# Expert slots in blocks of 32: seven groups of 128 in place of eight pairs and a part of 64

## The chip, the core and the metric

One NeuronCore of a Trainium2 chip runs the whole program in one launch. The metric is device time in microseconds of one execution. TensorE (PE, with its weight loads as PEld), VectorE (DVE), ScalarE (ACT), GpSimd (POOL) and SyncE (SP) each work through their own queue in order; 16 DMA engines move data between HBM and SBUF. Most loads are issued from SyncE's queue, a few from GpSimd's and ScalarE's.

## What is computed

Two residual layers over 256 tokens of width 1024 and a final RMSNorm. Each layer has a mixer (attention) and a mixture of 16 experts of hidden width 512, of which every token takes two. All is float32. The part that the change touches, from the reference:

```
aff = sigmoid(xf @ router_w)                       # 256 x 16
# per token: the best of 4 groups of 4 experts, in it the best 2 experts, weights w normed to 1
...
hid = silu(xb @ w_gate[e]) * (xb @ w_up[e])        # 1024 -> 512, for the tokens xb of expert e
ys  = hid @ w_down[e]                              # 512 -> 1024
out = out.at[tok].add(ys * w)                      # then x = x + gate_f * out
```

An expert has three matrices of 2 MB; all 16 are read in both layers, 100.7 MB a layer. How many tokens an expert gets depends on the data.

## The kernel before

`moe` (L957) runs once a layer, as the second half. It makes the router's values on DVE, and for each token and expert a position among the expert's tokens (`pos`) and a weight (`Wt`), both in `route` (L1030).

**Slots.** Every expert gets CAP = 64 slots. `pick` (L1042) compares `pos` with 0 to 63 and so makes a 0/1 matrix tokens x slots. `gather` (L1050) multiplies it with the tokens (8 chunks of 128 features, four matmuls each) and writes the gathered, scaled tokens to `XG`; it works for four experts (a quad, 256 columns) at a time. One expert of the first twelve, that with most tokens, is exchanged by `places` (L1348) for expert 4 (BIG) and gets 64 slots more, as a part of its own: `XG_x`, `x_hidden` (L1300), `x_slots`, `x_transposed`, `x_down` (L1328), worked in pair 4 (`self.more`, L1202). `rounds` (L1382) works out which tokens are still over, and `rest` (L1441) holds a conditional on their number: each round would load one expert's weights again for 64 tokens. `rest` reserves six ring tiles for that (L1442) and branches on PE, ACT, DVE and SP.

**Pairs.** Experts are worked in eight pairs (L1193), 64 slots of one on PSUM partitions 0 to 63, of the other on 64 to 127, so that a matmul has 64 columns of weights (the gathered tokens) and streams 512 columns of an expert's matrix. A pair does `hidden` (gate, then up, `gate_up` L1084: 8 chunks x 2 sides x 2 matrices), `slots` (`by_slot` L1111: transposes the 0/1 matrix to `OT` and brings the token weights to the slots), `turn` (`transposed` L1102), and, after the `hidden` of the next pair, `rows` (`down` L1135, then the weighting `rows_of` L1140); `combine` (L1128) adds the result to X. Each float32 matmul stands in the trace as two records. The very last pair ends with `finish` (L1272) in three pieces of columns, with the final norm behind them.

**Order and loads.** The loop at L1460 goes over the pairs; quads are gathered while pairs before them are worked. The conditional stands ahead of pair 4. Weights come in tiles of 1 MB into a ring of 15 slots (RING + EXTRA, L28): a pair has four tiles for gate, four for up and four for down. The program's order of loads is gate and up of a pair, then down of the pair before. Pairs 0 and 1 are always experts 12 to 15, so that their loads are issued without knowing the routing; the experts of later pairs are read from `ex_p` (L1346) into a register of SyncE (pair 4: of GpSimd, L1205), behind which SyncE's later loads stand. A scheduler orders each engine's instructions when the program is built; nothing passes the conditional.

**The shape with 32 columns** is in the program already: `ada_chunk` (L312) multiplies with weights of 32 columns, on the four quarters of a bank in turn (L322).

Of the kernel before, what the change touches and what calls it, by code (L numbers as in the profile page):

```python
# [29 lines left out]
QUADS = 3, 2, 1, 0  # L30
BIG = 4 * QUADS[2]


def shape_constants():
# [40 lines left out]
    iota = np.tile(1000 + np.arange(64, dtype=f)[None], (P, 1))  # L75
# [4 lines left out]
    sets = [[("ident", ident), ("iota", iota), ("rank", rank), ("sel", sel)],  # L80
# [17 lines left out]
def trunk(ctx, tc, ins, out):  # L98
# [858 lines left out]
    def moe(cp, wk, layer, norm, end):  # L957
# [73 lines left out]
        pos, Wt, cnt, ids = route[:, 0:2], route[:, 2:4], route[:, 4], route[:, 5]  # L1031
# [10 lines left out]
        def pick(o, at):  # L1042

            n = at.shape[2]
            iota = const("iota")[:, 0:CAP].unsqueeze(1).to_broadcast([P, n, CAP])
            for t in range(2):
                vec.tensor_tensor(o[:, t].rearrange("p (e s) -> p e s", e=n), iota,
                                  at[:, t].unsqueeze(2).to_broadcast([P, n, CAP]), ALU.is_equal)

        def gather(parts, o):  # L1050

            n = sum(m for _, m in parts)
            for k in range(8):
# [4 lines left out]
                at = 0  # L1058
                for XG, m in parts:
                    if (k + at // 256) % 2:  # L1060
                        act.activation(XG[:, k, :], b[:, at:at + m], AF.Identity, bias=sh[:, k:k + 1], scale=fa[:, k:k + 1])  # L1061
                    else:
                        vec.tensor_scalar(XG[:, k, :], b[:, at:at + m], fa[:, k:k + 1], sh[:, k:k + 1], ALU.mult, ALU.add)
                    at += m
# [15 lines left out]


        sides_ = (1, 0)

        def gate_up(XG, c0, Wg, Wu):  # L1084
# [93 lines left out]
        def pick_tile():  # L1178
            return wk.tile([P, 2, 6 * CAP], F32R, tag="pick", name="pick")

        def picked(q):
            o = pick_tile()
            pick(o[:, :, 0:4 * CAP], pos[:, :, 4 * q:4 * q + 4])
            if q == BIG // 4:
                pick(o[:, :, 4 * CAP:6 * CAP], at_b.unsqueeze(2).to_broadcast([P, 2, 2]))
            return o, q == BIG // 4

        def gathered(o, big_):
            XG = hp.tile([P, 8, 4 * CAP], F32, tag="HT", name="XG")
            gather([(XG, 4 * CAP)] + [(XG_x, CAP)] * big_, o)  # L1190
            return o, XG

        class Pair:  # L1193


            def __init__(self, i, o, XG):
                q, pp = QUADS[i // 2], i % 2
                self.first, self.last = i == 0, (layer, i) == (1, 7)
                self.after = i == 4
                self.o, self.XG, self.pp = o, XG, pp  # L1200
                self.e0 = 4 * q + 2 * pp
# [7 lines left out]
            def hidden(self):  # L1209
                names = ("moe_w_gate", "moe_w_up")  # L1210
                if self.first:
                    W = [load_both(nm, self.e0) for nm in names]
# [559 lines left out]
```

## Time and profile before

| | us |
|---|---|
| runs shown (3): lowest, median, highest | 897.03, 897.13, 898.13 |
| the profiled execution | 896.29 |
| its span, first to last instruction | 894.6 |
| busy: PE, PEld | 809.9, 417.0 |
| busy: DVE, ACT, POOL | 402.7, 250.2, 114.2 |
| moved by DMA | 291.09 MB, mean 325 GB/s |

All times in the text are microseconds from the start of the span of this one execution. A busy engine works on an instruction; matmuls overlap, and the end of each is modelled. Layer 0's experts run from about 227 to 490, layer 1's from about 632 to the end.

### The profile page before, as it was taken

Reading aid. Unit: us, or ns where it says so; the run is one execution under the profiler, and the core shown is the slowest. Engines: PE = TensorE matmul, PEld = TensorE weight load, DVE = VectorE, ACT = ScalarE, POOL = GpSimd, SP = SyncE. Lnnn points to the kernel's source line nnn. Section 1 sums busy time; section 2 is a strip of 40 time slices with the busy share of each in tenths; the row PEclk is TensorE's granted clock in tenths of the full one; section 3 lists DMA queues with packets and bytes.
Section 4 is the critical chain, followed back from the end, with each engine's and each line's share of the span. In section 5 each row is a group of like instructions: output and inputs, shape, how many; then the busy total and the mean of one; then the engine's idle time right before and its main releaser. Section 6 shows DMA issues by size and latency. Waiting matters only on the chain. (4 is left out here: it accounts for less than half of the span.)

```text
span 894.6 us, 12020 instructions
## 1 busy us (share of the span) xinstructions
PE 809.9 (91%) x4371; PEld 417.0 (47%) x4371; DVE 402.7 (45%) x1119; ACT 250.2 (28%) x595; POOL 114.2 (13%) x118
## 2 busy tenths in 40 slices
PE   4699999998999887999998799887999987999996
PEld 1298666555434333434332568555434333434333
DVE  2385777777623213124225754876613314115214
ACT  1264555545102001102012354546102112002113
POOL 1020211233000001000001223444000001000001
PEclk9799999998999998999999999989899999999998
DMA  9999869789899956999997977729699977999951
GB/s 326 343 342 386 301 233 272 282 310 368 314 421 400 406 205 253 419 419 420 397 406 257 337 267 204 297 104 362 226 421 421 419 282 280 419 418 419 415 197 47
DMA packets 84840, 291.09 MB, mean 325 GB/s; under 512 B 9174, under 2 KB 23202, under 8 KB 63010
## 3 DMA queue, kind: packets, MB, share of 16 engines
q1 hardware_dynamic: 76976, 258.36, 76.1%
q0 software_dynamic: 4608, 29.37, 8.5%
q10 hardware_dynamic: 3186, 2.47, 0.9%
q8 instruction: 38, 0.62, 0.3%
q14 instruction: 32, 0.26, 0.1%
HBM read 289.12 MB, written 1.06 MB: 324 GB/s over the span
## 5 line engine op out<-in xcount | busy, mean ns | idle before, releaser
L1078 PE MATMUL o<-slot,hT 128*64 128x512 f32 (+1 forms) x368 | 103.2, 611 | 7.7 <-PEq L1449 7.7
L1078 PE MATMUL mm<-slot,XG 128*64 128x512 f32 x328 | 94.2, 606 | 0.0
L1078 PE MATMUL sc<-slot,XG 128*64 128x512 f32 x352 | 90.4, 593 | 0.0
L1099 DVE TENSOR_TENSOR hq<-sc,hid 128x512 f32<-128x512 f32 x16 | 16.9, 1054 | 157.8 <-PE sc L1078 157.8
L497 ACT CAST hl<-slot 128x512 fp32r<-128x512 f32 (+2 forms) x112 | 60.7, 557 | 72.2 <-PE mm L514 45.3
L454 POOL TENSOR_TENSOR hl<-slot,hl 128x512 fp32r<-128x512 f32 x40 | 52.9, 1325 | 162.3 <-ACT hl L497 134.5
L1125 ACT CAST yg<-adac 128x512 fp32r<-128x512 f32 (+1 forms) x34 | 20.9, 613 | 148.3 <-DVE adac L1144 116.9
L1078 PE MATMUL mm<-room,XG 128*64 128x512 f32 x184 | 60.2, 606 | 0.0
L1144 DVE SCALAR_TENSOR_TENSOR adac<-o,w,GATE 128x512 f32<-128x512 f32 (+1 forms) x33 | 24.2, 735 | 77.8 <-PE o L1078 76.0
L1133 DVE TENSOR_TENSOR X<-X,tp 128x512 f32<-128x512 f32 (+1 forms) x72 | 46.2, 677 | 27.5 <-PE tp L1132 27.5
L1078 PEld LDWEIGHTS o<-slot,hT 128*64 128x64 f32 x368 | 31.8, 143 | 55.5 <-issue 51.5
L512 PE MATMUL mm<-HH,hl 128*128 128x256 f32 x176 | 54.5, 311 | 2.3 <-ACT HH L486 2.3
L322 PE MATMUL tp<-slot,csil 128*32 128x512 f32 x344 | 49.7, 655 | 3.7 <-DMA slot<-in_ada_w_dram 3.4
L1078 PEld LDWEIGHTS sc<-slot,XG 128*64 128x64 f32 x352 | 28.7, 137 | 51.3 <-issue 49.8
L1078 PE MATMUL o<-room,hT 128*64 128x512 f32 (+1 forms) x160 | 52.2, 575 | 0.0
L514 PE MATMUL mm<-HH,hl 128*128 128x256 f32 x176 | 50.2, 287 | 0.5 <-DVE hl L454 0.5
L513 PE MATMUL mm<-HH,hl 128*128 128x256 f32 x176 | 50.5, 288 | 0.1
L1132 PE MATMUL tp<-yg,OT 128*128 128x512 f32 (+1 forms) x128 | 42.6, 439 | 8.0 <-ACT yg L1125 4.2
L454 DVE TENSOR_TENSOR hl<-slot,hl 128x512 fp32r<-128x512 f32 (+2 forms) x72 | 42.8, 613 | 15.4 <-ACT hl L497 15.1
L1057 PE MATMUL tp<-pick,XH 128*128 128x256 f32 (+1 forms) x128 | 39.6, 333 | 10.6 <-ACT hT L1108 3.5
L1078 PE MATMUL sc<-room,XG 128*64 128x512 f32 x160 | 46.6, 592 | 0.0
L1057 PEld LDWEIGHTS tp<-pick,XH 128*128 128x128 f32 x128 | 24.5, 192 | 33.7 <-ACT XG L1061 6.7
(410 smaller groups left out, 1377.9 us busy)
## 6 DMA issues: line engine op xcount, KB each, us to landing
slot<-in_ada_w_dram SPq DMA_DIRECT2D x43, 1024.0 KB, 9.5
slot<-in_moe_w_down_dram SPq DMA_DIRECT2D x39, 1024.0 KB, 12.8
slot<-in_moe_w_gate_dram SPq DMA_DIRECT2D x37, 1024.0 KB, 12.7
slot<-in_moe_w_up_dram SPq DMA_DIRECT2D x35, 1024.0 KB, 10.3
room<-in_moe_w_gate_dram SPq DMA_DIRECT2D x19, 1024.0 KB, 9.4
room<-in_moe_w_up_dram SPq DMA_DIRECT2D x19, 1024.0 KB, 11.3
room<-in_moe_w_down_dram SPq DMA_DIRECT2D x13, 1024.0 KB, 10.5
slot<-in_ev_w_in_dram SPq DMA_DIRECT2D x8, 1024.0 KB, 10.2
```

The costliest lines, as they stand in the source:

```text
L322: mm(b[g:g + 32], csil[:, k, 1 - half:33 - half], W[k], start=k < 4, stop=k >= 4)
L454: eng.tensor_tensor(lo, v, hi.bitcast(F32), ALU.subtract)
L497: act.copy(hi, src)
L512: mm(o, a[0], b[0], start=start, stop=False, skip_group_check=True)
L513: mm(o, a[0], b[1], start=False, stop=False, skip_group_check=True)
L514: mm(o, a[1], b[0], start=False, stop=stop, skip_group_check=True)
L1057: mm(b, xk[i][:, t, k, :], o[:, t, 0:n], start=t == i == 0, stop=t == i == 1)
L1078: last[0] = mm(*args, **kw)
L1125: act.copy(yg[:, 0, :], v)
L1132: mm(cb, OT[:, t, :], x, start=i == 0, stop=i == 1)
L1133: vec.tensor_tensor(X[:, t, sl], X[:, t, sl], cb, ALU.add)
L1144: vec.scalar_tensor_tensor(v, y, w, gate[:, sl], ALU.mult, ALU.mult)
```

## The change

CAP stays for the rounds alone. Slots now come in blocks of 32. The first fourteen experts (0 to 13) are sorted on chip by their number of tokens (`places`): for every pair of them a comparison, a sum for the rank, and then six products and sums with a 0/1 matrix, which bring positions, weights, counts and numbers to sorted places (`placed`). The places have fixed sizes: the largest expert gets 96 slots, the next eight 64, the last five 32; experts 14 and 15 are not sorted and have 64. Seven groups of 128 slots take the places of the eight pairs: 14 + 15; 96 + 32; 64 + 32 + 32; 64 + 64; 64 + 32 + 32; 64 + 64; 64 + 64. A group with a 96 or a 32 is worked in four parts of 32 columns, one for each 32 partitions (`blocks`), where an expert of three blocks streams its matrix three times; the other groups are worked in two parts of 64, as before.

The part of 64 for the big expert goes out of the pairs; its functions stay for the rounds. The first gather covers group 0 alone (128 columns) and uses unsorted positions, the later ones two groups each (256 columns). Only group 0's experts are fixed; from group 1 on they are read from `ex_p`. `rounds` stands behind group 0; the conditional stands ahead of group 3 and follows a group of three experts. A load of a group of three experts has six tiles per matrix. The first set of constants has 78 columns more.

The diff, cut to its core:

```
+GROUPS = [[(14, 2), (15, 2)], [(0, 3), (1, 1)], [(2, 2), (3, 1), (4, 1)], [(5, 2), (6, 2)], [(7, 2), (8, 1), (9, 1)],
+          [(10, 2), (11, 2)], [(12, 2), (13, 2)]]
+RANKS = 0, 9, 1, 10, 11, 2, 3, 4, 12, 13, 5, 6, 7, 8
+SORTED = len(RANKS)
+BLOCK = 32
...
+        def blocks(group):
+            ns = [n for _, n in group]
+            if ns == [2, 2]:
+                return [(1, slice(64, 128)), (0, slice(0, 64))]
+            at = [a for a, n in enumerate(ns) for _ in range(n)]
+            return [(at[j], slice(BLOCK * j, BLOCK * j + BLOCK)) for j in reversed(range(4))]
+
+        def gate_up(XG, c0, parts, Wg, Wu):
...
-                    for a in sides_:
-                        put(b[64 * a:64 * a + 64], XG[:, k, c0 + a * CAP:c0 + (a + 1) * CAP], W[a][k], start=k == 0, stop=k == 7)
+                    for a, at in parts:
+                        put(b[at], XG[:, k, c0 + at.start:c0 + at.stop], W[a][k], start=k == 0, stop=k == 7)
...
-        def down(put, y, hT, Wd, k, half):
-            for a in sides_:
-                at = slice(64 * a, 64 * a + 64)
+        def down(put, parts, y, hT, Wd, k, half):
+            for a, at in parts:
...
-                self.more = self.e0 == BIG
-                es = [self.e0, self.e0 + 1]
-                if i > 1:
+                es = list(range(self.p0, self.p0 + self.n))
+                if i:
                     es = [load_value(ex_p[:, e:e + 1], [(ET.SP, ET.Pool)[self.after]], NE - 1) for e in es]
...
-                self.hid = gate_up(self.XG, 2 * CAP * self.pp, *W)
-                if self.more:
-                    self.hx = x_hidden(XG_x, [w[0] for w in W])
+                self.hid = gate_up(self.XG, self.c0, self.parts, *W)
...
-                    vec.tensor_copy(self.w[0:64], wb[0:64, 0:1])
-                    vec.tensor_copy(self.w[64:128], wb[64:128, 1:2])
+                    junk = wk.tile([P, 3], F32, tag="wj", name="wj")[:, 0:self.n]
+                    vec.tensor_tensor_reduce(out=junk, in0=wb, in1=self.owner, scale=1.0, scalar=0.0, op0=ALU.mult,
+                                             op1=ALU.add, accum_out=self.w)
...
-                if self.more:
-                    flush()
-                    late.extend(x_down(self.hTx, self.Wd[0]))
...
+            key = cp.tile([P, n], F32, name="key")
+            vec.scalar_tensor_tensor(key, route[:, 4, 0:n], 16.0, ids[:, 0:n], ALU.mult, ALU.add)
...
+            vec.tensor_tensor(more, key.unsqueeze(1).to_broadcast(wide), key.unsqueeze(2).to_broadcast(wide), ALU.is_gt)
+            rank = cp.tile([P, n], F32, name="rank")
+            vec.tensor_reduce(rank, more, AX.X, ALU.add)
+            vec.tensor_tensor(here, rank.unsqueeze(1).to_broadcast(wide), const("ranks").unsqueeze(2).to_broadcast(wide),
+                              ALU.is_equal)
+            for i in (5, 4, 0, 1, 2, 3):
+                vec.tensor_tensor(more, route[:, i, 0:n].unsqueeze(1).to_broadcast(wide), here, ALU.mult)
+                vec.tensor_reduce(placed[:, i, 0:n], more, AX.X, ALU.add)
+                if i == 5:
+                    vec.tensor_copy(ex_p[:, 0:n], placed[0:1, 5, 0:n])
...
-        now = gathered(*picked(QUADS[0]))
+        o, XG = gathered(*picked([0], route[:, 0:2]))
+        places()
         for h in range(2):
             vec.tensor_scalar(OT_x[:, h], ident.unsqueeze(1).to_broadcast([P, 2, P]), 0.0, None, ALU.mult)
-        at_b = places()
-        rounds()
+        then = picked([1, 2], placed[:, 0:2])
         before = None
-        for i in range(8):
-            p = Pair(i, *now)
-            if i == 4:
+        for i in range(len(GROUPS)):
+            p = Group(i, o, XG, 128 * (i > 0 and i % 2 == 0))
+            if i == 3:
...
-            if i % 2 == 0 and i < 6:
-                o = picked(QUADS[i // 2 + 1])
-            if i % 2 and i < 7:
-                now = gathered(*o)
+            if i % 2 == 0 and i < 5:
+                o, XG = gathered(*then)
+            elif i < 5:
+                then = picked([i + 2, i + 3], placed[:, 0:2])
+            if i == 0:
+                rounds()
```

## Rows read from the trace of the kernel before

**Rows 1.** The page: busy tenths of PE in 40 equal slices of the span (22.4 us each), and what the DMA engines moved in each.

```profile
PE   4699999998999887999998799887999987999996
GB/s 326 343 342 386 301 233 272 282 310 368 314 421 400 406 205 253 419 419 420 397 406 257 337 267 204 297 104 362 226 421 421 419 282 280 419 418 419 415 197 47
```

**Rows 2.** Busy time by stretch: the expert stages up to the branch, from the branch to the landing of the last expert weight, and behind it. Columns: the stretch and its length; busy us (and instructions) of PE, PEld, DVE, ACT, POOL; granted clock of PE; share of the DMA engines; GB/s.

```profile
227.10:351.30 124.20, 109.96 (x512) 45.54 (x513) 39.26 (x105) 17.64 (x34) 2.74 (x5) 0.98 0.84 332
351.30:464.40 113.10, 111.49 (x550) 45.55 (x552) 28.64 (x51) 14.23 (x26) 3.90 (x8) 0.98 1.00 407
464.40:490.00 25.60, 21.92 (x98) 7.64 (x98) 11.62 (x18) 4.00 (x9) 4.95 (x15) 1.00 0.87 301
631.60:749.80 118.20, 107.68 (x515) 45.62 (x514) 39.33 (x105) 17.73 (x34) 2.74 (x5) 0.99 0.84 338
749.80:863.50 113.70, 112.00 (x554) 45.01 (x554) 29.55 (x52) 14.34 (x26) 3.70 (x7) 0.99 1.00 402
863.50:894.60 31.10, 22.34 (x108) 9.46 (x108) 12.75 (x26) 7.75 (x22) 3.88 (x4) 0.91 0.09 35
```

**Rows 3.** SyncE's last issue of an expert load in layer 0 (timeline), its time to landing, and the time to landing of all expert loads of L1160 (minimum, median, maximum).

```profile
454.39 0.33 SPq L1160 DMA_DIRECT2D room<-in_moe_w_down_dram  x1
DMA to landing us min/median/max: 10.0/10.0/10.0
DMA to landing us min/median/max: 5.0/11.5/25.9
```

**Rows 4.** Busy time by stretch (columns as in rows 2) in layer 1, ten us before the branch's end and ten us soon after.

```profile
740.00:750.00 10.00, 5.59 (x22) 3.23 (x24) 4.79 (x11) 1.94 (x4) 0.14 (x1) 0.96 0.47 196
760.00:770.00 10.00, 10.00 (x66) 4.71 (x64) 1.28 (x3) 0.90 (x3) 1.02 (x2) 1.00 1.01 418
```

**Rows 5.** Who waited for whom, PE alone: us in total, times, longest.

```profile
PE o L1078 <- PEq L1449: 7.7, 2, 4.2
PE tp L322 <- DMA slot<-in_ada_w_dram: 3.4, 4, 1.5
```

**Rows 6.** Timeline around layer 0's branch: issues of loads by SyncE (SPq) and GpSimd (POOL). Start, length, what, and for how long and by what the queue stood before it.

```profile
314.92 0.33 SPq L1160 DMA_DIRECT2D slot<-in_moe_w_down_dram  x1
339.35 0.53 POOL L1160 DMA_DIRECT2D slot<-in_moe_w_up_dram  x1
351.40 1.19 POOL L1160 DMA_DIRECT2D slot<-in_moe_w_up_dram  x2 [11.53 <-PEq L1449]
```

**Rows 7.** The chain that ended last, in order of time: one up phase of a pair in layer 1.

```profile
791.53 6.87 PE sc L1078 x32
```

**Rows 8.** Timeline of PE: one `ada_chunk` at the full clock.

```profile
129.74 1.92 PE L322 MATMUL tp<-slot,csil 128*32 128x512 f32 x16
```

**Rows 9.** Busy time in layer 0's stretch up to the branch, of one line's instructions each (PE, then PEld; clock, DMA share, GB/s of the stretch): L1078 (gate, up, down), L1057 (gather), L1132 (combine), L1116 (transposes of slots), L1118 (weights of slots), L1106 (transposes of the hidden values).

```profile
227.10:351.30 124.20, 80.38 (x352) 24.05 (x353) 0.98 0.84 332
227.10:351.30 124.20, 17.87 (x96) 13.17 (x96) 0.98 0.84 332
227.10:351.30 124.20, 8.59 (x24) 3.93 (x24) 0.98 0.84 332
227.10:351.30 124.20, 1.75 (x8) 0.80 (x8) 0.98 0.84 332
227.10:351.30 124.20, 2.02 (x16) 2.10 (x16) 0.98 0.84 332
227.10:351.30 124.20, 2.59 (x16) 1.68 (x16) 0.98 0.84 332
```

**Rows 10.** The branch instructions of the conditional's line on PE's sequencer, two layers: minimum, median and maximum in ns.

```profile
L1449 PEldq COMPARE_BRANCH  x2: 3391/3616/3842, 347.2 to 746.1; - x2
```

**Rows 11.** Layer 0 from the branch to the end of the stage: busy time of L1306 (gate and up of the part of 64) and of L1333 (its down), and the group of its combine (busy us, mean ns of one; idle before).

```profile
351.30:490.00 138.70, 8.45 (x64) 5.14 (x64) 0.98 0.97 387
351.30:490.00 138.70, 5.16 (x16) 1.06 (x16) 0.98 0.97 387
L1132 PE MATMUL tp<-yg,OT_x 128*128 128x512 f32 x8 | 2.4, 420 | 0.0
```

**Rows 12.** Timeline: the last down record of layer 0 on PE and the last two additions to X on DVE; the last piece's matmuls of layer 1.

```profile
484.35 0.59 PE L1078 MATMUL o<-slot,hT 128*64 128x512 f32 x1
488.66 1.29 DVE L1133 TENSOR_TENSOR X<-X,tp 128x512 f32<-128x512 f32 x2 [0.30 <-PE tp L1132]
883.32 1.95 PE L1078 MATMUL o<-room,hT 128*64 128x256 f32 x16
```

**Rows 13.** From layer 0's last expert landing to the first product of layer 1's attention: the stretch (columns as in rows 2), and that product in PE's timeline.

```profile
464.40:501.00 36.60, 29.48 (x143) 10.71 (x140) 21.34 (x39) 8.67 (x19) 6.22 (x16) 1.00 0.86 290
501.02 0.47 PE L512 MATMUL o<-hl,HH 128*128 128x512 f32 x1 [1.58 <-ACT hl L497]
```

**Rows 14.** Timeline of DVE in layer 0: the key, a product on 96 elements, a comparison on 256, and the experts' numbers.

```profile
226.30 0.17 DVE L1357 SCALAR_TENSOR_TENSOR key<-route 128x16 f32<-128x16 f32 x1
228.61 0.26 DVE L1366 TENSOR_TENSOR here<-route,is_max 128x96 f32<-128x96 f32 x1
230.38 0.42 DVE L1047 TENSOR_TENSOR pick<-K,route 128x256 fp32r<-128x256 f32 x1
230.71 0.16 DVE L1372 CAST ex_p<-route 1x16 int32<-1x16 f32 x1
```

**Rows 15.** Busy time by stretch (columns as in rows 2): just behind layer 0's branch.

```profile
351.30:354.00 2.70, 2.69 (x8) 0.94 (x10) 0.60 (x2) 0.00 (x0) 1.59 (x3) 0.50 0.49 109
```

More of the change, by code (lines that the diff above doesn't have):

```diff
@@ L74, in shape_constants @@
     sin = np.tile(np.sin(ang).T, (4, 1)).astype(f)
-    iota = np.tile(1000 + np.arange(64, dtype=f)[None], (P, 1))
+    iota = np.tile(1000 + np.arange(96, dtype=f)[None], (P, 1))
+    ranks = np.tile(np.array(RANKS, f)[None], (P, 1))
+    places = sorted(x for g in GROUPS for x in g)
+    size = np.tile(np.array([BLOCK * n for _, n in places], f)[None], (P, 1))
+    owner = np.concatenate([np.repeat(np.eye(len(g), dtype=f), [BLOCK * n for _, n in g], axis=0) for g in GROUPS], axis=1)
     rank = np.tile((4 - np.arange(4)).astype(f)[None], (P, 1))
@@ L1040, in moe, with pick, gather @@
         gate = GATE[5]
[L1042 removed]
+        def pick(o, at, m):
             n = at.shape[2]
[L1045 removed]
+            iota = const("iota")[:, 0:m].unsqueeze(1).to_broadcast([P, n, m])
             for t in range(2):
                 vec.tensor_tensor(o[:, t].rearrange("p (e s) -> p e s", e=n), iota,
[L1048 to L1052 removed]
+                                  at[:, t].unsqueeze(2).to_broadcast([P, n, m]), ALU.is_equal)
+        def gather(XG, n, o):
             for k in range(8):
@@ L1178, in pick_tile, with picked, gathered, __init__ @@
         def pick_tile():
-            return wk.tile([P, 2, 6 * CAP], F32R, tag="pick", name="pick")
-        def picked(q):
+            return wk.tile([P, 2, 256], F32R, tag="pick", name="pick")
+        def picked(groups, pos):
             o = pick_tile()
[L1183 to L1190, printed above, removed]
-            return o, XG
[L1193 to L1201, printed above, removed]
-                self.more = self.e0 == BIG
-                es = [self.e0, self.e0 + 1]
-                if i > 1:
+            places, at = [x for g in groups for x in GROUPS[g]], 0
+            while places:
+                p0, m = places[0]
+                n = 1
+                while n < len(places) and places[n] == (p0 + n, m):
+                    n += 1
+                pick(o[:, :, at:at + n * m * BLOCK], pos[:, :, p0:p0 + n], m * BLOCK)
+                at += n * m * BLOCK
+                places = places[n:]
+            return o, at
+        def gathered(o, n):
+            XG = hp.tile([P, 8, n], F32, tag="HT", name="XG")
+            gather(XG, n, o)
+            return o, XG
+        class Group:
+            def __init__(self, i, o, XG, c0):
+                self.first, self.last = i == 0, (layer, i) == (1, len(GROUPS) - 1)
+                self.after = i == 3
+                self.o, self.XG, self.c0 = o, XG, c0
+                self.p0, self.n = GROUPS[i][0][0], len(GROUPS[i])
+                self.parts = blocks(GROUPS[i])
+                first = sum(len(g) for g in GROUPS[:i])
+                self.owner = const("owner")[:, first:first + self.n]
+                es = list(range(self.p0, self.p0 + self.n))
+                if i:
                     es = [load_value(ex_p[:, e:e + 1], [(ET.SP, ET.Pool)[self.after]], NE - 1) for e in es]
@@ L1211, in hidden @@
                 if self.first:
-                    W = [load_both(nm, self.e0) for nm in names]
+                    W = [load_both(nm, self.p0) for nm in names]
                 else:
@@ L1294, in moe @@
         NR = 7
-        XG_x = cp.tile([P, 8, CAP], F32, name="XG_x")
         w_x = cp.tile([P, 1], F32, name="w_x")
@@ L1346, in moe @@
         ex_p = cp.tile([1, 16], I32, name="ex_p")
+        placed = cp.tile([P, 6, 16], F32, name="placed")
         def places():
@@ L1358, in places @@
-            vec.memset(is_max, 0.0)
-            free = slice(0, 4 * QUADS[0])
-            vec.tensor_reduce(top_, key[:, free], AX.X, ALU.max)
-            vec.tensor_scalar(is_max[:, free], key[:, free], top_, None, ALU.is_equal)
-            a, b = (cp.tile([P, NR, 16], F32, tag=n, name=n)[:, 0:6] for n in ("here", "here_t"))
-            col = cp.tile([P, 6], F32, name="xcol")
-            wide = is_max.unsqueeze(1).to_broadcast([P, 6, 16])
-            vec.tensor_tensor(a, route, wide, ALU.mult)
@@ L1375, in places @@
-            return at
+            n = SORTED
+            key = cp.tile([P, n], F32, name="key")
+            vec.scalar_tensor_tensor(key, route[:, 4, 0:n], 16.0, ids[:, 0:n], ALU.mult, ALU.add)
+            wide = [P, n, n]
+            more, here = (x[:, 0:n * n].rearrange("p (a b) -> p a b", b=n) for x in (ada_tile(), ada_tile()))
+            vec.tensor_tensor(more, key.unsqueeze(1).to_broadcast(wide), key.unsqueeze(2).to_broadcast(wide), ALU.is_gt)
+            rank = cp.tile([P, n], F32, name="rank")
@@ L1378, in moe @@
+            vec.tensor_copy(placed[:, :, n:16], route[:, :, n:16])
         at_x = cp.tile([P, 2, NR], F32, name="at_x")
@@ L1465, in moe @@
                 rest()
-            if i == 7 and layer:
+            if p.last:
                 end.load()
```

54 lines of the change are left out of this document (16 added, 38 removed).

## The prediction

> **What bounds the kernel now.** I read the slices of the page first [rows 1]: the long stretches where the DMA engines move some 419 GB/s are the two expert stages, and there PE is at nine tenths as well. Busy PE says little, so I cut each stage at its one conditional (`rest`, L1441) and took a table of stretches [rows 2]. The two layers are twins: 124.2 and 118.2 us up to the branch at 332 and 338 GB/s, then 113.1 and 113.7 us to the landing of the last expert weight at 407 and 402 GB/s, then a tail without expert loads of 25.6 us (to the end of the stage in layer 0) and 31.1 us (to the end of the span in layer 1). In layer 0 the landing is 454.4 + 10.0, issue and time to landing of the last load [rows 3]; in layer 1 the stretch behind 863.5 moves 35 GB/s, the 1 MB of the output. In the tens around the branch [rows 4] the loads fall to less than half and return to 418 GB/s for good.
>
> Which of PE and DMA holds each part is read from PE's waits [rows 5]: the list of what PE waited for names loads of `ada_w` (and one constant at the start), never a load of an expert; the expert stage's largest wait is the branch itself. So up to the branch PE is the bound, and the DMA queue waits for PE to free slots. After it the two are matched: DMA is full, and PE has so much queued that it ends 20 us and more after the last landing.
>
> Why DMA sags is seen in the issues [rows 6]: SyncE issues its last load before the branch at 314.92; GpSimd then gets out five tiles, the fifth at 339.35, and the sixth goes at 351.40, released by the branch. The ring has 15 slots, `rest` holds 6 through the branch (L1442) and the previous pair's down weights 4; five are left.
>
> **What the change takes away.** Tokens first, since slots must hold them: the routing of the reference on its inputs gives layer 0 a largest expert of 58 tokens, layer 1 of 71 (expert 0), then 57 (expert 2). Of the fourteen sorted ones ranks 9 to 13 have at most 26 and 20 tokens, experts 14 and 15 at most 30. All fit 96, 64 and 32 slots, so `rest` runs no round, and the trace of before shows none either (no instruction of L1430 to L1439).
>
> One matrix phase (gate, up or down of 128 slots) is 32 matmul records in 6.87 us, two in each 0.43 [rows 7]. Will a group of four 32-slot parts take the same? It has 64 records, in four column groups. The trace has that shape: `ada_chunk` (L322) runs 16 records of 128 rows x 32 columns x 512 in 1.92 us [rows 8]; less the 0.16 us by which a record outlasts its spacing (0.59 [rows 12], against 0.43) that is 0.11 us a record, and 64 make 7.0. I take 6.87; bounds 6.87 and, if only two of the four ran at once, 13.74.
>
> Before the branch: four pairs become three groups, so gate, up and one down go: 3 x 6.87 = 20.6 us. The gathers (L1057, 17.87 us) cover 128 + 256 + 256 in place of 256 + 256 + 320 columns: 17.87 x 192/832 = 4.1. One combine of three: 8.59/3 = 2.9. One of four of the slot transposes, slot weights and hidden transposes: (1.75 + 2.02 + 2.59)/4 = 1.6 [rows 9]. Together 29.2 us a layer. The 14.2 us in which PE was idle there (124.2 - 110.0, [rows 2]) and the 3.4 to 3.8 us of the branch [rows 10] I leave as they are.
>
> After the branch: the overflow part of the big expert goes, 8.45 + 5.16 + 2.4 = 16.0 us [rows 11] and its small transposes. PE's count of pairs stays (four gates, four ups, five downs), so PE needs about 139 - 16 = 123 us there in layer 0.
>
> **What it adds, and what is late next.** A layer has 96 tiles of 1.05 MB. Before, 4 pairs (48 tiles) and GpSimd's five are issued by the branch, and 43 remain: 45.1 MB, and the stretch shows 113.1 x 0.407 = 46.0. After, groups 0 to 2 hold seven experts (42 tiles), and the ring has 15 - 6 - 6 = 3 slots for group 3, so 51 remain: eight more, at 2.50 us each (1.05 MB at 419 GB/s) 20.0 us. From the branch to the last landing thus 133.1 and 133.7 us, more than PE's 123: the second part is held by DMA. Last landing: 29.2 - 20.0 = 9.2 us earlier in each layer.
>
> The tail shrinks, because PE waits for the last tile in place of holding a queue. Layer 0: the last two tiles feed half a down phase (3.43), and from its end (484.94) to the last addition to X (489.95) are 5.0 us [rows 12]: 8.4 for 25.6, that is 17.2 less. Layer 1: half of the last piece (0.97), then from the piece's end (885.27) to the end of the span 9.3: 10.3 for 31.1, 20.8 less. If PE still has a few us queued, that much is lost; bounds 0 and 4 us a layer.
>
> Between the layers a cover goes. The next layer's `ada` and attention weights now land while PE ends layer 0: 36.6 us x 290 GB/s = 10.6 MB from the last expert landing to the first attention product at 501.02 [rows 13]. After, that time is 8.4 + 11.0 = 19.4 us, 8.1 MB at 419; missing are 2.5 MB, 6.0 us. Bounds: 0 (not all of it is wanted by the first product) and 10.0 (all that landed by 490, 7.7 MB, is wanted 8.4 us after the last landing). I take 6.0, since that product is the first to need the new weights.
>
> The sort adds a wait. Before, the eight tiles of pair 0 and seven of pair 1 are loaded ahead of the routing; after, only experts 14 and 15 are fixed, and SyncE's queue stands at group 1's expert numbers, with all later loads behind it. Those come from `ex_p`, which was ready at 230.71 + 0.16, some 4.6 us after its key, after ten small steps among other work [rows 14]. The new chain has compare, sum, equality, product, sum on 196 elements; 96 elements took 0.26 us and 256 took 0.42, so about 0.36 each, 1.8 us together. I keep 231. An expert load landed 5.0 us after its issue at least [rows 3]. If not even group 0's down tiles go ahead, 88 remain: 232 + 5 + 87 x 2.5 = 454.5, against 464.4 - 9.2 = 455.2 from the branch. So this wait costs nothing yet, and each us by which the sort is later costs nearly one in each layer. With the four down tiles ahead there are 10 us of room.
>
> Small things at nothing: `rounds` (some 35 steps of 0.15 to 0.28 us on DVE) moves past group 0; only `rest` waits for it, 80 us on. Sorted weights and positions (eight products and sums, 2.9 us) are wanted by the second gather, some 12 us after the routing; without that cover 2.9 us a layer. Four more register loads stand on SyncE, which idles. 78 more constant columns are 40 KB, 0.1 us.
>
> **Sum**, against the profiled execution of 896.29 us (span 894.6): layer 0 -9.2 - 17.2, layer 1 -9.2 - 20.8, between them +6.0: -50.4, so 845.9. The median of the runs shown is 897.13, 0.84 above it, so I say 846.5.
>
> **Rivals.** (a) Weights late: the sort is placed behind the gather's evacuations on DVE, or SyncE stands at the register load with group 0's down tiles behind it. With the numbers 10 us later, both layers end 9.3 us later: 865. For it: the queue is in order, and 17 us of loads no longer lie ahead of the routing. Against: the steps are short.
>
> (b) Slower: the four parts don't run at once. Place: the phases of groups 1, 2 and 4, five before the branch, four after. At 13.74 us a phase the branch comes 34.4 later and PE needs 123 + 27.5 = 150 us after it: with the branch 5.2 later (34.4 - 29.2) and 150 in place of 139 that is 17 us more a layer, 930. It decides from 5 us more a phase (those before the branch, ten in two layers, then eat 50), 0.19 us a record in place of 0.107. Against it stands the one row of [rows 8].
>
> (c) The same place at a part of the price: parts of a group share the array, but with losses of 2 us a phase: ten on the path, 867. The same row speaks against it, though there the four parts stream four different weights, while the 96-slot expert streams one tile three times at once. The Trainium skill, "TensorE: Matmul & The Clock Gate", part 3, "Measured speedup vs the span model", gives 2.38 for three column tiles and 3.07 for four row tiles. By 3.07 in place of 4 a phase would be 8.95 us, and the sum 20.8 us higher, some 867; the trace's 16 records in 1.92 us don't agree.
>
> (d) No change: the branch comes no earlier because the 28 tiles that groups 1 and 2 and two downs need before it (70 us from the sort) are late by 25 us. I see nothing for that.
>
> PE's clock falls where it waits: behind the branch the granted clock was 0.50, the lower of its two levels (1.2 of 2.4 GHz) [rows 15]. Groups of three wait about 45 - 28 us for weights; at half clock their phases still fit the 45. Only the last half phase of a layer can pay, 3.4 us; that is in the tail's bound.
>
> **Numbers.** Forecast 846.5, alone within 833 to 860 (gather and idle time +-3 us a layer, tail 0 to +4 a layer, between the layers -6 to +4): 0.68. (a) 0.15, (c) 0.08, (b) 0.06, (d) 0.03. The range reaches to (a) and (c): 829 to 870. A measurement here tells 0.2% from no change; faster 0.91, same 0.03, slower 0.06.
>
> **What would show it.** The branch at some 322 and 700 in place of 351 and 750; no sag of DMA around it; from the branch to the last landing 133 us at 419 GB/s; PE waiting for expert weights, which it never did; tails near 8 and 10 us; 64 records of 32 columns in 6.9 us; `ex_p` ready within 6 us of its key. Wrong would be me if those phases took 9 us or more, if DMA stood idle for over 15 us at the first group, or if the branch came less than 20 us earlier.

## The result, and the profile after

868.88 us in place of 897.31 (medians of four runs each on one chip): ratio 0.968, 95% interval 0.9663 to 0.9697, 28.4 us faster. The forecast was 846.5 within 829 to 870; so the sign and the range hold, and 22 us of the 50 did not come. The narrower interval that the forecast gave to its own mechanism, 833 to 860, was missed by 9 us. The profiled execution took 869.42 us, span 867.2.

The page's slices, 21.7 us each, to be held against [rows 1]: the sag around the branch has shrunk to one slice a layer (337 and 361 GB/s), and a hole stands ahead of each layer's experts: 96 GB/s in slice 11, and 122 and 179 in slices 28 and 29 (in the kernel before, one such slice, 104, stood ahead of layer 1's).

```profile
PE   4699999999799969759997899979899967769996
GB/s 328 349 328 387 321 248 217 280 376 219 96 422 418 419 417 337 419 420 419 419 415 389 360 350 196 288 130 122 179 419 419 419 361 395 420 420 419 416 396 77
```

Busy time by stretch, columns as in [rows 2]: in each layer from the key of the sort to PE's first record behind the branch, from there to the last landing of an expert weight, and behind it.

```profile
227.42:324.90 97.48, 86.06 (x560) 37.95 (x559) 33.89 (x105) 13.20 (x25) 1.69 (x3) 0.92 0.96 393
324.90:464.30 139.40, 117.18 (x632) 40.02 (x632) 28.91 (x50) 14.21 (x26) 7.13 (x15) 0.92 0.98 404
464.30:473.00 8.70, 6.91 (x32) 2.50 (x36) 5.27 (x9) 2.13 (x5) 2.83 (x10) 1.00 1.04 386
613.62:710.22 96.60, 85.81 (x561) 37.84 (x560) 33.87 (x105) 13.20 (x25) 1.69 (x3) 0.92 0.96 393
710.22:848.90 138.68, 116.79 (x621) 39.52 (x622) 27.69 (x48) 14.21 (x26) 4.78 (x9) 0.92 0.98 397
848.90:867.20 18.30, 10.61 (x60) 5.47 (x59) 8.41 (x19) 5.92 (x18) 3.89 (x4) 0.85 0.15 58
```

With the same points in the kernel before (keys at 226.30 and 630.81, the rest in [rows 2, 12]) the 27.4 us of span divide as follows:

| | forecast | measured |
|---|---|---|
| start to layer 0's key | 0 | +1.1 |
| layer 0, key to branch | -29.2 | 125.0 to 97.5: -27.5 |
| branch to last landing | +20.0 | 113.1 to 139.4: +26.3 |
| landing to end of stage | -17.2 | 25.6 to 8.7: -16.9 |
| to layer 1's key | +6.0 | 140.9 to 140.6: -0.2 |
| layer 1, key to branch | -29.2 | 119.0 to 96.6: -22.4 |
| branch to last landing | +20.0 | 113.7 to 138.7: +25.0 |
| landing to end | -20.8 | 31.1 to 18.3: -12.8 |

Three rows were forecast about right (layer 0 to the branch, layer 0's tail, the start). The misses are 6.3 and 5.0 us behind the branches, 6.8 before layer 1's, 8.0 in the last tail, and 6.2 the other way between the layers.

The numbers of the experts came when forecast: timeline of DVE in layer 0, the key, the first step on 196 elements, and the cast to `ex_p` (to be held against [rows 14]; start, length, engine, line, what).

```profile
227.42 0.17 DVE L1366 SCALAR_TENSOR_TENSOR key<-route 128x14 f32<-128x14 f32 x1
228.18 0.35 DVE L1369 TENSOR_TENSOR adac<-key 128x196 f32<-128x196 f32 x1
230.98 0.16 DVE L1378 CAST ex_p<-placed 1x14 int32<-1x14 f32 x1
```

But SyncE had nothing left to load. Its timeline: the last tiles of group 0's up, then nothing until `ex_p`; the stretches between, of layer 0 and layer 1, move 11 and 1 GB/s. Group 0's down tiles were not among what went ahead. The prediction had named this as a sign of being wrong, the DMA engines idle for over 15 us at the first group, and it came in both layers.

```profile
201.10 1.58 SPq L1185 DMA_DIRECT2D slot<-in_moe_w_up_dram  x2
231.94 1.91 SPq L1171 DMA_DIRECT2D slot<-in_moe_w_gate_dram  x3
```

```profile
213.00:231.94 18.94, 13.38 (x79) 8.01 (x78) 13.85 (x55) 8.62 (x11) 6.23 (x2) 0.77 0.03 11
602.00:617.98 15.98, 12.11 (x61) 6.02 (x60) 12.88 (x48) 7.31 (x9) 5.95 (x2) 0.72 0.00 1
```

PE's waits (us in total, times, longest), to be held against [rows 5]: PE now waits for expert weights, above all for up, and longer at the branch.

```profile
PE sc L1084 <- DMA slot<-in_moe_w_up_dram: 13.6, 5, 6.7
PE o L1084 <- PEq L1453: 13.1, 2, 6.8
PE sc L1084 <- DMA room<-in_moe_w_up_dram: 8.3, 1, 8.3
PE mm L1084 <- DMA room<-in_moe_w_gate_dram: 5.6, 2, 4.3
```

### The profile page after: what moved, and what is told of

Its sections match the earlier page's. It is cut to its first block, busy times and chain, and to the rows that moved or that the text cites. A ratio compares the mean times of both kernels' runs of the same rounds, so it can differ in the third digit from the quotient of the medians.

```text
span 867.2 us, 12251 instructions
## 1 busy us (share of the span) xinstructions
PE 746.6 (86%) x4499; PEld 381.9 (44%) x4499; DVE 377.8 (44%) x1091; ACT 237.4 (27%) x569; POOL 115.6 (13%) x118
## 5 line engine op out<-in xcount | busy, mean ns | idle before, releaser
L1084 PE MATMUL o<-slot,hT 128*32 128x512 f32 (+2 forms) x448 | 93.5, 619 | 14.0 <-PEq L1453 13.1
L1084 PE MATMUL sc<-slot,XG 128*64 128x512 f32 (+1 forms) x416 | 92.1, 646 | 13.6 <-DMA slot<-in_moe_w_up_dram 13.6
L1084 PE MATMUL mm<-slot,XG 128*32 128x512 f32 (+1 forms) x416 | 85.9, 624 | 5.2 <-DMA slot<-in_moe_w_gate_dram 5.2
L1084 PE MATMUL mm<-room,XG 128*64 128x512 f32 (+1 forms) x224 | 57.1, 629 | 5.6 <-DMA room<-in_moe_w_gate_dram 5.6
L1084 PE MATMUL o<-room,hT 128*32 128x512 f32 (+2 forms) x208 | 58.6, 603 | 2.0 <-DMA room<-in_moe_w_down_dram 2.0
L1084 PEld LDWEIGHTS sc<-slot,XG 128*64 128x64 f32 (+1 forms) x416 | 25.3, 132 | 70.1 <-issue 48.6
L1084 PE MATMUL sc<-room,XG 128*32 128x512 f32 (+1 forms) x224 | 45.0, 656 | 8.3 <-DMA room<-in_moe_w_up_dram 8.3
L1068 ACT ACTIVATE XG<-tp,mod,mod 128x256 f32<-128x256 f32 (+1 forms) x32 | 17.2, 538 | 124.0 <-PE tp L1066 124.0
L1084 PEld LDWEIGHTS o<-slot,hT 128*32 128x32 f32 (+1 forms) x448 | 25.5, 125 | 54.3 <-issue 36.0
L464 DVE TENSOR_TENSOR hl<-slot,hl 128x512 fp32r<-128x512 f32 (+2 forms) x72 | 42.6, 611 | 15.3 <-ACT hl L507 15.0
L1145 DVE TENSOR_TENSOR X<-X,tp 128x512 f32<-128x512 f32 (+1 forms) x56 | 36.0, 675 | 16.5 <-PE tp L1144 16.2
## 6 DMA issues: line engine op xcount, KB each, us to landing
slot<-in_ada_w_dram SPq DMA_DIRECT2D x43, 1024.0 KB, 10.3
slot<-in_moe_w_gate_dram SPq DMA_DIRECT2D x37, 1024.0 KB, 15.1
```

Source lines behind the costliest of these rows:

```text
L464: eng.tensor_tensor(lo, v, hi.bitcast(F32), ALU.subtract)
L1068: act.activation(XG[:, k, :], b, AF.Identity, bias=sh[:, k:k + 1], scale=fa[:, k:k + 1])
L1084: last[0] = mm(*args, **kw)
L1145: vec.tensor_tensor(X[:, t, sl], X[:, t, sl], cb, ALU.add)
```

## Experiments

First theories. **D:** a layer's experts are one queue of loads, 88 tiles from the numbers on, so what moves loads moves the time. **P:** what is missing lies on PE (half clock, a longer branch). After four runs neither stood alone, and a third took their place, **two limits**: loads and PE's chain lie within a few us of each other, and both must move.

Each kernel is the changed one with the edit shown, cut to its core. The table gives, from the profiles, the us from `ex_p`'s cast (its end) to the last expert landing and to PE's last down record, layer 0 / layer 1. Ratios are to the kernel before, on the same chip.

| kernel | numbers to landing | numbers to PE's last down | us | ratio, interval |
|---|---|---|---|---|
| changed | 233.2 / 231.6 | 236.9 / 240.5 | 868.88 | 0.968, 0.9663 to 0.9697 |
| e1 | 232.4 / 230.1 | 236.1 / 238.3 | 866.0 | 0.9641, 0.9612 to 0.9671 |
| e2 | 233.3 / 231.8 | 237.0 / 240.0 | 878.07 | 0.9769, 0.9744 to 0.9793 |
| e3 | 231.3 / 230.4 | 235.0 / 239.0 | 864.87 | 0.9624, 0.9601 to 0.9648 |
| e5 | 235.9 / 229.0 | 241.3 / 237.3 | 866.12 | 0.9641, 0.9605 to 0.9677 |
| e6 | 237.4 / 235.3 | 241.1 / 243.4 | 876.64 | 0.9767, 0.9736 to 0.9798 |
| e8 | 232.2 / 229.6 | 235.9 / 239.0 | 869.4 | 0.9676, 0.9652 to 0.9701 |
| e9 | 232.7 / 231.9 | 237.4 / 242.6 | 869.26 | 0.9671, 0.9643 to 0.9699 |
| e10 | 234.1 / 233.8 | 237.7 / 243.9 | 878.29 | 0.9774, 0.9744 to 0.9803 |
| e11 | 218.3 / 222.8 | 238.7 / 240.4 | 869.19 | 0.9673, 0.9651 to 0.9694 |
| e12 | 219.2 / 219.8 | 230.6 / 232.5 | 856.39 | 0.9535, 0.9506 to 0.9564 |
| e13 | 223.4 / 221.9 | 227.1 / 227.9 | 845.87 | 0.9409, 0.9388 to 0.9431 |
| e14 | 222.4 / 224.6 | 241.7 / 240.1 | 868.96 | 0.9671, 0.9649 to 0.9694 |

**e1, early down tiles.**

```
             p.hidden()
+            if i == 0:
+                p.load_down()
```

> The down tiles of group 0 are asked for right behind its gate and up, ahead of SyncE's stand at the expert numbers. Theory D: from the numbers to the last landing the stage is one queue of 88 tiles of 2.50 us; four of them now land in the idle time before, so the last landing comes 10 us earlier in each layer and the time falls by 16 to 20 us, to some 849 to 853. Theory P (what is missing of the forecast is PE at half clock and the longer branch): no change, 869.

Neither. The ratio's interval touches that of the changed kernel, and the landing is 0.8 and 1.5 us earlier, not 10. The four tiles did land in the hole; but then the loads thinned out, in two stretches of 10 us in which PE was busy throughout: SyncE stood at 279.07 for 11 us behind PE's up matmuls, for a slot that they had yet to free.

```profile
260.00:270.00 10.00, 10.00 (x80) 3.50 (x80) 0.54 (x1) 1.16 (x2) 0.00 (x0) 1.00 0.79 277
270.00:280.00 10.00, 10.00 (x76) 2.55 (x68) 2.29 (x3) 0.62 (x1) 0.00 (x0) 1.00 0.57 238
```

**e2, late numbers.**

```
-            for i in (5, 4, 0, 1, 2, 3):
+            for i in (4, 0, 1, 2, 3, 5):
```

> The experts' numbers are made last of the six sorted rows in place of first: five products and five sums of 0.35 us and the work between them put ex_p some 4.5 us later, everything else is as it was. Theory D: every us counts in full, twice 4.5: +9 us, 878. Theory P: the first gather and gate need no number, at most +1 us, 869 to 870.

As D: in layer 0 `ex_p` is at 236.32 in place of 231.14 and the branch 5.2 us later; the ratio is 0.9769 for 0.968, some 8 us for two layers' 10. So earlier loads gain little and later ones cost most of their delay: each limit holds on its own side.

**e3, no conditional.**

```
                 flush()
-                rest()
```

> Leaves out the rounds for tokens that find no slot (there are none in this data), so there is no conditional and nothing is held for it. Theory D: the DMA engines lose 14 us x (1 - 287/419) = 4.4 us at each conditional, where SyncE waits until all that it issued has landed; without it the last landing is 4.4 us earlier in each layer, 860. Theory P: PE's two waits of 13.1 us go and with them the half clock behind, 3.3 and 3.6 us: 849.

Neither: 864.87 is above both, some 5 us under the changed kernel by the ratios. In the landing it is 1.9 and 1.2 us, not 4.4: the stop of the loads at the branch is mostly made up. The edit also gives back the six ring slots, so these figures are the price of both.

**e5, two fixed groups.**

```
+GROUPS = [[(12, 2), (13, 2)], [(14, 2), (15, 2)], [(0, 3), (1, 1)], [(2, 2), (3, 2)], [(4, 2), (5, 1), (6, 1)],
+          [(7, 2), (8, 1), (9, 1)], [(10, 2), (11, 2)]]
+RANKS = 0, 7, 1, 2, 3, 8, 9, 4, 10, 11, 5, 6
```

> Experts 12 to 15 are fixed, in two groups of 64 + 64; twelve are sorted, with one of 96, six of 64 and five of 32 slots, still seven groups of 128; the four-part groups are 2, 4 and 5, the conditional follows a group of two experts. Fifteen tiles are ahead of the numbers. Theory D: 81 tiles remain, and the first of them waits for the first gate (some 240 in layer 0): 240 + 81 x 2.5 + 4.4 + 5.3 = 452 in place of 464.3 for the last landing, -12 us a layer: 845 to 849. Theory P: 869, since PE's work is the same.

As P, near enough: the fifteen tiles ahead didn't shorten layer 0 at all. Only six experts, not seven, are worked before the branch, so more of the loads fall behind it.

**e6, down tiles of group 2 by GpSimd.**

```
+                if i == 2:
+                    self.es_d = [load_value(ex_p[:, e:e + 1], [ET.Pool], NE - 1) ...]
+                self.dq = (sp, pool)[i in (2, 3)]
-                    self.Wd = load_experts("moe_w_down", self.es, 4, queue=(sp, pool)[self.after])
+                    self.Wd = load_experts("moe_w_down", self.es_d, 4, queue=self.dq)
```

> The six down tiles of group 2, the last loads ahead of the conditional, are issued by GpSimd in place of SyncE, so that at the conditional SyncE has only loads outstanding that have landed long before. Theory D (SyncE's wait for its own landings stops the DMA engines at the conditional, and behind it they are the bound): the stop of 4.4 us goes, the last landing comes 4 us earlier in each layer, some 860 to 862. Rival: the stop is PE's branch itself, which holds the six slots until it is through: no change, 869, and GB/s at the branch as before.

Slower. With nothing of its own outstanding, SyncE still loaded next at 332.87, just ahead of PE's first record behind the branch (333.04): the rival, for this kernel. In the changed kernel it is the other way: PE goes on at 324.90, SyncE only at 329.38, 0.8 us behind the landing of its last own tile (issued at 300.85, landed 27.7 us later). So in these two kernels the loads waited for the later of the two. SyncE's timeline, the changed kernel, then e6:

```profile
329.38 7.72 SPq L1171 DMA_DIRECT2D room<-in_moe_w_gate_dram  x2
```

```profile
332.87 0.33 SPq L1171 DMA_DIRECT2D room<-in_moe_w_gate_dram  x1
```

And a new cost came: GpSimd's six tiles are wanted last, but landed between SyncE's four, which PE needed first. The larger groups of loads issued from 277 to 300, with their median time to landing; first the changed kernel, then e6.

```profile
slot<-in_moe_w_down_dram SPq DMA_DIRECT2D x6, 1024.0 KB, 21.8
room<-in_moe_w_down_dram SPq DMA_DIRECT2D x3, 1024.0 KB, 18.0
```

```profile
slot<-in_moe_w_down_dram POOLq DMA_DIRECT2D x5, 1024.0 KB, 17.2
room<-in_moe_w_down_dram SPq DMA_DIRECT2D x3, 1024.0 KB, 28.4
```

PE waited 6.34 us, to just behind the landing of SyncE's second tile (issued at 280.28, landed 27.3 us later); the profile puts the wait down to SyncE's branch line:

```profile
307.63 1.06 PE L1084 MATMUL o<-room,hT 128*32 128x512 f32 x1 [6.34 <-SPq L1457]
```

**e8, early down tiles and PE kept busy.** Beside e1's edit:

```
+        hot = bank("tp", [P, 512])
+        for _ in range(5):
+            mm(hot, ident, X[:, 0, 0:512], start=True, stop=True)
         pb = bank("sc", [P, 2, 16])
```

> Group 0's down tiles are asked for early, and five matmuls of 128 x 512 whose product is not used stand in PE's queue ahead of the routing's sums, where PE idled for 5.6 us. Theory two limits (up to the branch PE and the loads hold the time within 1 us of each other, PE because its first gather and first gate run at half clock): with both moved, the branch comes 4 to 6 us earlier than in the kernel with the early down tiles alone, and the time falls by 8 to 12 us from that kernel's 866.0, to 854 to 858. Theory that the clock there costs nothing: 866.

No gain, and not a clean test: the extra matmuls ran into the routing, so the numbers came 2.0 us later than in e1 in layer 0. PE came to the first gather at the full clock, yet its 32 matmuls took 7.3 us, as in the changed kernel. There PE works through them without a wait at 0.50, a record each 0.21 us; here they follow each other in 0.11 us at first, but PE waited for DVE, which was sorting beside its evacuations, and was busy for 5.9 of the 7.3 us; the granted clock fell again, to 0.79 over the gather and over the first gate. The stretch up to the gather, a matmul of it that waited, the gather, the first gate:

```profile
222.00:231.00 9.00, 8.13 (x45) 2.32 (x44) 6.63 (x30) 0.58 (x1) 0.00 (x0) 1.00 0.35 118
...
234.93 0.33 PE L1069 MATMUL tp<-pick,XH 128*128 128x128 f32 x1 [0.68 <-DVE XG L1073]
...
231.24:238.54 7.30, 5.91 (x35) 5.18 (x36) 7.04 (x29) 1.37 (x3) 0.00 (x0) 0.79 0.44 146
238.47:247.43 8.96, 8.96 (x35) 2.93 (x36) 5.99 (x34) 0.46 (x1) 0.00 (x0) 0.79 1.01 390
```

**e9, the end of layer 1.**

```
+                before.rows()
                 end.load()
             p.hidden()
-            if before is not None:
+            if before is not None and not p.last:
```

> In layer 1 the down phase of group 5, loads and matmuls, is put ahead of the gate and up of group 6. Theory tail (PE holds a whole down phase of 7.1 us when the last weights land, which is why the tail is 18.3 and not 10.3 us): the last landing stays, PE ends some 7 us earlier, 862. Rival: the tail is the last pieces' own chain of matmul, weighting, combine and norm, 869.

The rival's number. PE is behind in either order of its last phases: its last down record now ended at 860.21, 10.8 us after the last landing. **e10**, the four edits of e1, e6, e8 and e9 in one, carries e6's loss and tells nothing more.

> The four edits together: early down tiles of group 0, five matmuls in PE's idle time, group 2's down tiles by GpSimd, and group 5's down phase ahead of group 6. If each term is its own, the sum of 3 + 10 + 8 + 7 us: 841. If the limits only change places (loads behind the branch full from there to the end), the first two bring less: 850.

**e11 and e12, the place of the conditional.** Twelve experts sorted, both groups of three right behind the two fixed ones; in e12 the conditional is one group later still.

```
+GROUPS = [[(12, 2), (13, 2)], [(14, 2), (15, 2)], [(0, 2), (1, 1), (2, 1)], [(3, 2), (4, 1), (5, 1)], [(6, 3), (7, 1)],
+          [(8, 2), (9, 2)], [(10, 2), (11, 2)]]
+RANKS = 1, 7, 8, 2, 9, 10, 0, 11, 3, 4, 5, 6
-            if i == 3:
+            if i == 4:                  # e12: 5
```

> Experts 12 to 15 fixed as in the run with two fixed groups, but both groups of three experts stand right behind them, the group with the 96 slots follows, and the conditional stands ahead of group 5 of 7 (after ten experts, not six). Theory two limits (PE with the ring of 15 slots up to the conditional, the loads behind it): 30 tiles are asked for between the numbers and the conditional that fell behind it before; 81 tiles from 240, 4.4 and 5.3 us give 452 for layer 0's last landing, PE needs 235 + 7 x 28.3 + 6.9 = 440; 12 us a layer less, 846 to 850. If the order of the groups doesn't matter, as with the two fixed groups alone: 866.

> As the run before, with the conditional one group later, after twelve experts. Two limits: the same sums, 846 to 850, if PE keeps its pace; the stop of PE of 6.9 us now lies so near the end that it isn't made good in layer 1: up to 5 us more, 855.

e11: the loads came even earlier than expected (landing 447.02), but the time stayed: PE ended where it ended in the changed kernel, 20 us after the landing. e12 is the best that holds all of the computation: 42.6 us under the kernel before on its chip, ratio 0.9535, just above the 855 that stood as the upper end. PE's chain is 6 and 8 us shorter; in layer 0 it stands 9.6 us at the branch, but then waits for no up tile. PE's waits tell e11 and e12 apart: between the numbers and PE's last down record, by layer, it waits some 16 and 16 us for weights in e11 (18 and 17 in the changed kernel), and 4 and 5 in e12, while its busy time is 203 to 209 us in all three.

**e13, half of PE's work.** Beside e1's edit:

```
-                for k in range(8):
+                for k in range(0, 8, 2):
```

> Leaves out every other of the eight chunks in gate and up of all groups (half of these matmuls; all loads stay), and asks for group 0's down tiles early. Theory two limits: with PE halved, the ring is free in time, and the loads alone hold the stage: 84 tiles, so 10 us a layer less than with the early down tiles alone, and a shorter end: 840 to 848. Rival (the loads can't start earlier for another reason): 862 to 866.

As two limits: with PE relieved, the landing is 9.8 and 9.7 us earlier than in the changed kernel, where the same four early tiles alone (e1) brought 0.8 and 1.5, and the time is 845.87. What half of PE's work brings without the early tiles wasn't run, so the 9.8 us belong to the two together. Layer 1 behind its last landing:

```profile
828.86:844.19 15.33, 7.65 (x49) 4.16 (x48) 7.11 (x17) 5.92 (x18) 3.88 (x4) 0.86 0.18 68
```

**e14, e5 with the conditional ahead of group 5.**

```
-            if i == 3:
+            if i == 5:
```

> The kernel with experts 12 to 15 fixed and its order of groups (96 + 32, then 64 + 64, then the two groups of three experts, then 64 + 64), with one line moved: the conditional stands ahead of group 5, not 3. Two limits: with groups of two experts first (some 28 us of PE, 30 us of loads each) the ring stays full, the groups of three (45 us of loads) use up that lead, and neither waits long; 81 tiles from 240 give 452 to 457 for layer 0's last landing and PE ends 4 us behind it, 5 us a layer less than with the groups of three in front: 846 to 852. If the place of the conditional is not what cost the two fixed groups their lead: 866.

Missed: again an early landing (450.41) and an unmoved end. PE waits behind the branch, in layer 0 twice for group 5's up tiles. GpSimd had asked for them from 383.82 on; SyncE's tiles for group 6, which PE wants later, landed beside them.

```profile
411.24 5.87 PE L1084 MATMUL sc<-room,XG 128*32 128x512 f32 x32 [11.12 <-DMA room<-in_moe_w_up_dram]
425.92 5.36 PE L1084 MATMUL sc<-slot,XG 128*32 128x512 f32 x32 [8.81 <-DMA slot<-in_moe_w_up_dram]
```

```profile
room<-in_moe_w_up_dram POOLq DMA_DIRECT2D x3, 1024.0 KB, 17.6
slot<-in_moe_w_up_dram POOLq DMA_DIRECT2D x3, 1024.0 KB, 28.4
slot<-in_moe_w_gate_dram SPq DMA_DIRECT2D x2, 1024.0 KB, 10.1
room<-in_moe_w_gate_dram SPq DMA_DIRECT2D x2, 1024.0 KB, 16.3
```

That PE waits for tiles of one queue while those of another land beside them is shown in e6; that this alone holds the end in e11 and e14 is argued from these rows. The same loads on one queue weren't tried.

## Why the prediction was right and where it was wrong

**What was right, and what was luck.** Up to the branch PE was the limit (in layer 0 it waited there for weights for 0.9 us in all), and the fewer phases moved the branch by 27.5 us in layer 0. A phase in four parts costs what one in two parts costs: 32 records of 32 columns take 3.64 us, 16 of 64 columns 3.65, so rivals (b) and (c) are out.

```profile
343.81 3.65 PE L1084 MATMUL sc<-slot,XG 128*64 128x512 f32 x16 [1.77 <-DMA slot<-in_moe_w_up_dram]
365.17 3.64 PE L1084 MATMUL mm<-slot,XG 128*32 128x512 f32 x32
```

The sort cost what was forecast, `ex_p` 3.6 us after its key. Behind the branch the loads are the limit, and layer 0's tail is 8.7 us for 8.4. That the time lies within 829 to 870 is luck in part: the range went up to 870 for rivals (a) and (c), and neither late numbers nor slower phases came. What brought the time there were terms of the forecast with the wrong size, each below.

**Behind the branch: +26.3 and +25.0, not +20.0.** The step counted tiles not yet issued: 51 for 43. By bytes it is 139.4 x 404 less 113.1 x 407, 10.3 MB in layer 0, 138.7 x 397 less 113.7 x 402, 9.4 MB in layer 1, that is 24.6 and 22.3 us at 419 GB/s in place of eight tiles (8.4 MB); the rest, 1.7 and 2.7 us, is a lower rate. The surplus in bytes has two sources. What had been issued had not all landed at the branch: until the next issue 0.7 MB moved in layer 0 and 1.0 MB in layer 1 (before, nothing was left to land), which is all of layer 1's surplus. And in layer 0 a load of 1 MB for the next layer (`scr`), by GpSimd, now stands ahead of the last expert landing (464.30), where it stood behind it before (464.4). The two stretches from PE's first record to the next issue; that load after, then before:

```profile
324.90:329.33 4.43, 4.43 (x24) 1.24 (x28) 0.59 (x2) 0.00 (x0) 0.00 (x0) 0.53 0.39 159
710.22:715.09 4.87, 4.87 (x28) 1.36 (x32) 0.59 (x2) 0.00 (x0) 0.00 (x1) 0.53 0.50 205
```

```profile
447.56 0.93 POOL L407 DMA_DIRECT2D room<-scr  x1 [11.15 <-PE sc L1084]
```

```profile
465.82 0.93 POOL L397 DMA_DIRECT2D room<-scr  x1 [11.15 <-PE sc L1078]
```

"No sag of DMA around it" was wrong too: the loads stop there for PE and for SyncE's own landings (e6), though e3 puts the price at no more than 2 us a layer in the landing.

```profile
321.00:335.00 14.00, 10.10 (x66) 2.98 (x68) 1.79 (x4) 0.62 (x1) 2.65 (x5) 0.76 0.74 287
```

**Before the branch: 29.2 us of PE's work.** PE's busy time fell by 110.0 - 86.1 = 23.9 us in layer 0 and by 108.4 - 85.8 = 22.6 in layer 1. From key to branch in the kernel before:

```profile
226.30:351.31 125.01, 109.96 (x512) 45.55 (x513) 40.07 (x108) 17.64 (x34) 2.74 (x5) 0.98 0.84 333
630.81:749.77 118.96, 108.44 (x513) 45.59 (x513) 40.09 (x108) 17.73 (x34) 2.74 (x5) 0.99 0.84 336
```

In layer 0 less idle time (15.1 to 11.4) made up for most of what was missing, in layer 1 (10.5 to 10.8) nothing did. By lines, the phases as a whole (80.4 to 59.1 us and 79.1 to 58.9), the combines and the small transposes came out as forecast. The mis-sized term is the gather: it was scaled by its columns to 4.1 us less, but takes 18.1 us in both layers where it took 17.9 and 17.5, because the first one, of 128 columns, takes 7.2 us. After PE's wait in front of it the granted clock is at its lower level, 0.50, through that gather and into the first gate: 9.47 us for a phase of 6.87 [rows 7]. The clock isn't the gather's only limit: begun at 1.00 (e8) it took as long. The wait in PE's timeline, the gather and the gate of the changed kernel:

```profile
224.44 2.07 PE L301 MATMUL tp<-adac,HALF 128*128 128x512 f32 x2 [5.56 <-DVE adac L344]
```

```profile
228.32:235.55 7.23, 7.23 (x35) 7.04 (x36) 7.05 (x27) 1.37 (x3) 0.00 (x0) 0.50 0.37 116
235.48:244.95 9.47, 9.47 (x35) 3.03 (x36) 6.46 (x37) 0.46 (x1) 0.00 (x0) 0.74 1.01 426
```

That only the last half phase of a layer can pay for the clock was wrong. The branch took 2.6 and 2.7 us more as well.

**The numbers: "this wait costs nothing yet".** Borne out: the loads from the numbers on were a limit as near as PE. e2 shows that nearly nothing is left on the late side, e1 that only 1 us was to be had on the early one, not the "10 us of room". Both sums, 454.5 and 455.2 for the last landing, were some 9 us too low (464.30). Of rival (a) one half came, SyncE at the register load with group 0's down tiles behind it, and the other, numbers 10 us late, did not; that its 865 lies nearer than 846.5 does not speak for it.

**The last tail: 18.3 us, not 10.3.** It was taken as half of the last piece (0.97 us) and 9.3 us that follow. What follows took 9.4; from the last landing to PE's last down record it is 8.9 us in place of 0.97, because PE still has earlier pieces and their combines to do. With PE relieved (e13) the tail still is 15.3, so some 5 of the 8 us are work on the last pieces that stays then too; the other 3 are PE's backlog from earlier phases, within the 4 that stood as a bound. Once the weights have landed PE, not a load, holds the time:

```profile
850.00:860.00 10.00, 9.51 (x56) 4.89 (x52) 5.60 (x13) 3.75 (x13) 3.36 (x4) 1.00 0.00 1
```

**Between the layers: +6.0 did not come.** The first attention product follows the end of the stage by 11.1 us (484.08 after 473.00), as in the kernel before (501.02 after 489.95, [rows 12, 13]): that is the lower bound of that step. So not all that landed early before was wanted by this product.

```profile
484.08 0.47 PE L522 MATMUL o<-hl,HH 128*128 128x512 f32 x1 [1.58 <-ACT hl L507]
```

## What to carry to other kernels

Where a step is taken from the engine that is the limit, work out the next limit to the same precision: here loads and PE lay some 1 us apart, and the four kernels that brought loads forward and left PE late (e1, e5, e11, e14) gained 3.5 us at most by their ratios. At a barrier count the loads that have landed, not those that have been issued, and ask what else is issued before the last one lands. Ask in which order two queues deliver: counted from the numbers, e11 and e14 landed their last tile 7 to 15 us earlier and gained nothing. And a gather of half the columns isn't half the work when it comes right behind PE's wait: the first one took 7.2 us at the lower clock, and e8, which began it at the full clock, met DVE as the next limit.

## What the runs showed of the hardware

**The branch took longer while the loads ran at full rate.** The conditional's branch instruction on PE took 3.4 to 3.8 us before [rows 10], and 6.1 to 6.5 after:

```profile
L1453 PEldq COMPARE_BRANCH  x2: 6131/6292/6452, 318.1 to 703.8; - x2
```

In the thirteen kernels with a branch this goes with what the DMA engines moved meanwhile: 6.0 to 6.5 us in the eight where they moved 371 to 427 GB/s, 3.3 to 3.9 in the five (before, e5, e6, e10, e14) where they moved 6 to 105. The stretch of PE's wait in e11 and in e6 (layer 0):

```profile
347.85:354.27 6.42, 0.00 (x0) 0.03 (x1) 0.96 (x3) 0.00 (x0) 0.00 (x0) 0.59 1.01 422
```

```profile
328.87:333.04 4.17, 0.01 (x1) 0.03 (x1) 0.90 (x3) 0.00 (x0) 0.00 (x0) 1.00 0.03 6
```

No run took this by itself. In each of these branches the trace has a packet of 16 KB on the instruction queue q8: in e6, with nothing else on the way, 1.0 us after the branch's start in both layers, in the changed kernel 3.9 and 3.7 us after it. The Trainium skill, "Runtime: NRT & Kernel Launch", section "Instruction fetch mechanics", says that a taken branch out of the loaded window waits for a DMA fetch of its target; the trace agrees, but that the fetch waits its turn behind the loads is argued from these two times.

**Two queues share the DMA engines.** In e6 SyncE's down tiles took 28.4 us to land beside GpSimd's, in place of 18.0 (medians of two each). From 296 to 308, while both had loads on the way, SyncE's queue (q1) and GpSimd's (q0) moved as many packets each (packets, MB, share):

```profile
q1 hardware_dynamic: 347, 2.56, 51.6%
q0 software_dynamic: 347, 2.47, 49.5%
```

The Trainium skill, "DMA: Bandwidth & Descriptors", section "Queues, rings and completion order", has each engine go round its queues packet by packet; the equal counts agree.
